# One hybrid encoder layer: 1/rms of the tokens spread over partitions by DMA through DRAM instead of TensorE, and four weight splits held until a late matmul

## The chip, the cores and the metric

The kernel runs on one core of a Trainium2 chip. The metric is the device time of one execution in microseconds. An execution is profiled as well; its trace gives every instruction of the five engines (PE is TensorE's matmul, PEld its weight load, DVE VectorE, ACT ScalarE, POOL GpSimd) and the DMA traffic. SP's queue only issues DMAs.

## The reference

One layer on 1,024 tokens of width 1,024, all in float32:

```
h = rms_norm(x, norm1_g)
u = h @ w_in                                  # conv (a, gate), q, k, v, g
a_out = conv_group(a * sigmoid(gate))         # causal depthwise conv(31), layer norm, silu
b_out = retention(rotary(q), rotary(k), v)    # chunked, 4 heads of 128, rms norm, * silu(g)
x = x + concat([a_out, b_out]) @ w_out
x = x + relu(rms_norm(x, norm2_g) @ w_ff1)**2 @ w_ff2
return rms_norm(x, final_g)
```

`rms_norm` multiplies each token by 1/sqrt(mean of its squares + eps). That one number per token is what the first part of the change moves about.

## The kernel before, in words

Each float32 matrix product is made of three products of rounded halves (`mm3`, L149 to L151): every operand is split into a high part `hi` (ACT copies it to the rounded type) and a low part `lo` (DVE subtracts). So each weight block needs one ACT and one DVE instruction before PE can use it. For w_in and w_out a block is loaded into `raw` (a pool of two buffers, L112), and split into `w` (L116 and L117, or L126 and L127 where a scale is multiplied in).

The tokens are not normalised before the first projection. x arrives transposed (`xcol`), is multiplied by norm1_g and split, and the factor 1/rms of a token, `r1`, is applied to the results. `stats` (L259 to L267) gets it: a block of 128 tokens `xt` is loaded with a token on each partition, ACT squares and sums it, POOL adds eps and takes the power -0.5. Where a result has tokens on partitions (q, k, v, g), `r1` is used as it is. The convolution's inputs (the gate tiles, `glu_proj` and `glu_gate`) have channels on partitions and tokens along the row, so there the factors have to stand as a row, the same on all 128 partitions: `r1_row`, one tile `row` of 128x512 for each half of the tokens. The kernel makes it with PE: POOL multiplies the identity by `r1` (`diag`, L351), PE multiplies by a matrix of ones (`pb`, L352), and ACT copies PSUM to `row` (L354). `pb` takes two buffers of the PSUM pool `pr` (four banks).

`glu_gate` does, for each half: `zg` (DVE, L294, accumulator times row), `sg` (ACT, sigmoid), `sr` (POOL, times row), `glu` (DVE, L299). It frees the PSUM banks of its gate tile. Four gate tiles j = 0 to 3 of 128 channels are made; j = 0 and 1 come first, then the projection of v (`wv`), then tiles 2 and 3, then k and q. The two half-tiles of j = 1 take banks of `pr`, those of j = 0 banks of `ps` (four banks), and the first group of v takes banks of `ps` that j = 0 held.

The convolution is 31 multiply-adds per channel tile on DVE (`y`, L395), spread over the whole first half of the kernel: each is put behind a matmul in the order of the program by a table (QUOTA). Such an entry, and `hold`, sets the order in which the scheduler places instructions; it adds no wait on the chip.

Retention handles the token blocks in pairs (`retention`, L438 to L480): PE transposes k and q (`pk`, `pq`), adds k times v to the running `pstate`, which ACT copies to `state` (L456) before the next block may add to it, makes the scores `psc` (L460), which DVE masks into `sT` (L462), and multiplies by v (`po`, L466 and L468). Between, PE works on the projection groups of q and of the gate g (`wg`, four groups of two blocks). The output projection starts with the retention half: `wo`, four row blocks of w_out multiplied by ret_norm_g (`load_wo(NC, True)`), then the convolution half `woa`.

The rest (feed-forward by a Strassen scheme) is not touched. Every engine carries out its instructions in order; an instruction that waits holds up what is queued behind it. `n2d` (L339) is a small DRAM tensor: SP's queue writes norm2_g to it, 1,024 separate numbers of 4 bytes, and `n2row` reads it back spread over the partitions.

Of the kernel before, what the change touches and what calls it, by code (L numbers as in the profile page):

```python
# [8 lines left out]
F32 = mybir.dt.float32  # L9
F32R = mybir.dt.float32r  # L10
BF16 = mybir.dt.bfloat16
AF = mybir.ActivationFunctionType
ALU = mybir.AluOpType
PSUM = bass.MemoryType.PSUM

P = 128
D = 1024
S = 1024
# [9 lines left out]
NC = CW // P  # L28
NF = FF // P
HALF = 512  # L30
# [11 lines left out]
def hybrid_layer_kernel(  # L42
# [14 lines left out]
    nc = tc.nc  # L57
# [6 lines left out]
    sp = pool("sp", 11)  # L64
    tiny = pool("tiny", 8)
    xd = pool("xd", 1, space=bass.MemoryType.DRAM)
# [3 lines left out]
    pr = pool("pr", 4, space=PSUM)  # L70
# [10 lines left out]
    ones = const.tile([P, P], F32, name="ones")  # L81
    nc.vector.memset(ones, 1.0)
    ident = const.tile([P, P], F32, name="ident")
# [12 lines left out]
    col = lambda nm, i: vec[:, cols[nm] + i : cols[nm] + i + 1]  # L96
# [9 lines left out]
    def load_raw(src, spare=False):  # L106

        if spare:
            raw = cp.tile(list(src.shape), F32, tag="c", name="raw")
        else:  # L110
            raw = rawp.tile(list(src.shape), F32, tag="raw", name="raw")
        nc.sync.dma_start(raw, src)  # L112
        return raw

    def split_row(raw, w, i):
        nc.scalar.activation(w[:, 0, i], raw[:, i], AF.Copy)  # L116
        nc.vector.tensor_tensor(w[:, 1, i], raw[:, i], w[:, 0, i].bitcast(F32), ALU.subtract)  # L117

    def split(raw, scales):

        w = wp.tile([P, 2] + list(raw.shape[1:]), F32R, tag="w", name="w")
        for i in range(raw.shape[1]) if scales else [slice(None)]:
            if scales is None:
                split_row(raw, w, i)
            else:
                nc.scalar.activation(w[:, 0, i], raw[:, i], AF.Copy, scale=scales[i])  # L126
                nc.vector.scalar_tensor_tensor(  # L127
                    w[:, 1, i], raw[:, i], scales[i], w[:, 0, i].bitcast(F32), ALU.mult, ALU.subtract
                )
        return w  # L130

    def load_split(src, scales):
        return split(load_raw(src), scales)

    pe_log, tap_log, act_log = [], [], []

    def hold(ins, until):

        name = lambda i: i.ins if hasattr(i, "ins") else i
        tc.add_manual_dep(  # L140
            name(ins),
            name(until).name,
            mybir.DependencyInfo(mybir.DependencyClass.NoSync, mybir.DependencyReason.DATA),
            reason="others first",
        )
# [15 lines left out]
    def mean_sq(src):  # L161

        tr = sp.tile([P, D], BF16, tag="s", name="trash")
        ss = tiny.tile([P, 1], F32, tag="ss1", name="ss")
        nc.scalar.activation(tr, src, AF.Square, scale=D**-0.5, accum_out=ss)
        return ss
# [43 lines left out]
    def chunk_w(c):  # L210
        return [load_split(w_in[c, i], None) for i in range(ND // 2)]
# [7 lines left out]
    def bank(i):  # L219

        if i % 2:
            return pr.tile([P, HALF], F32, tag="r", name="acc")
        return ps.tile([P, HALF], F32, tag="mm", name="acc")

    def proj_group(w, blocks, i=0):
        accs = [bank(i) for _ in blocks]
        for d in range(ND):
            for a, b in zip(accs, blocks):
                proj_tokens(w, b, a, d, d == 0, d == ND - 1)
        return accs  # L230

    r1, r1_pair = {}, None
# [22 lines left out]
    def stats(t):  # L255

        nonlocal r1_pair
        xt = cp.tile([P, D], F32, tag="c", name="xt")
        nc.sync.dma_start(xt, x[t * P : (t + 1) * P, :])  # L259
        if t % 2 == 0 or t >= 4:  # L260
            r1_pair = const.tile([P, 2], F32, name=f"r1_{t}")
            r1[t] = r1_pair[:, 0:1]
        else:
            r1[t] = r1_pair[:, 1:2]
        m = tiny.tile([P, 1], F32, tag="nmr", name="m1")
        nc.gpsimd.tensor_tensor(m, mean_sq(xt), eps1, ALU.add)
        nc.gpsimd.tensor_tensor(r1[t], m, mhalf[:, 0:1], ALU.pow)  # L267


    def glu_accs(j):  # L270
# [2 lines left out]
    def glu_proj(w, j, accs, d, h):  # L273

        for q in range(2):
            lo = (2 * j + q) * P
            mm3(
                accs[q][h],
                w[d // 2][:, 0, d % 2, lo : lo + P],
                w[d // 2][:, 1, d % 2, lo : lo + P],  # L280
                hT.half(d, 0, h),
                hT.half(d, 1, h),
                d == 0,
                d == ND - 1,
            )
# [31 lines left out]
    w = []  # L317
    accs = glu_accs(0)
    with tc.manual_schedule(engines=ordered):
# [6 lines left out]
        for i in range(ND // 2):  # L326
# [5 lines left out]
            for h in range(2):  # L332
                for d in (2 * i, 2 * i + 1):
                    glu_proj(w, 0, accs, d, h)
    nc.sync.dma_start(dec, decay)
    for t in range(NB):
        stats(t)
    n2d = xd.tile([D], F32, name="n2d")
# [2 lines left out]
    first, accs = accs, [[bank(1)], [bank(1)]]  # L341
# [3 lines left out]

    r1_row = []
    for h in range(2):
        pb = pr.tile([P, 4, P], F32, tag="r", name="pb")
        for i in range(4):
            diag = sp.tile([P, P], F32, tag="s", name="diag")  # L350
            nc.gpsimd.tensor_scalar(diag, ident, r1[4 * h + i], None, ALU.mult)  # L351
            nc.tensor.matmul(pb[:, i], lhsT=ones, rhs=diag, start=True, stop=True)  # L352
        row = sp.tile([P, HALF], F32, tag="s", name="row")
        nc.scalar.activation(row, pb.rearrange("p i t -> p (i t)"), AF.Copy)  # L354
        r1_row.append(row)
    nc.sync.dma_start(trg, trig)

# [16 lines left out]
    for g in range(NG):  # L374
        if g == NG - 1:
            w = chunk_w(2)
# [39 lines left out]
    w = wk  # L416
# [66 lines left out]
    def retain(waiting):  # L483
        runs = [retention(b, qr) for b, qr in waiting]
        for _ in range(3):
            for run in runs:
                next(run)
# [9 lines left out]

    marks.append(len(pe_log))

    def load_wo(first, scales):  # L500
        return [
            load_split(w_out[first + c].unsqueeze(1), [col("rg", c)] if scales else None) for c in range(NC)
        ]


# [20 lines left out]
    def ret_side(b):  # L526

        xr = [sp.tile([P, HALF], F32, tag="s", name="xr") for _ in range(2)]
        for n in range(2):
            nc.sync.dma_start(xr[n], x[b * P : (b + 1) * P, n * HALF : (n + 1) * HALF])  # L530
        pt = pr.tile([P, NC, P], F32, tag="r", name="pt")
        for c in range(NC):
            nc.tensor.transpose(out=pt[:, c], in_=blk[b][:, 0, c * P : (c + 1) * P], identity=ident)
        return split_tiles(pt), xr

    rsides = {}
    for g in range(NG):
        if g == NG - 1:
            wo = load_wo(NC, True)
        blocks = range(GB * g, GB * g + GB)  # L540
        accs = proj_group(wg, blocks)
        retain(waiting)
        waiting = []
        for b, acc in zip(blocks, accs):
            sg = sp.tile([P, CW], F32, tag="s", name="sg")
            nc.scalar.activation(sg, acc, AF.Silu, scale=r1[b])
            nc.vector.tensor_tensor(blk[b][:, 0], blk[b][:, 0], sg, ALU.mult)
            if b in (4, 5):
                rsides[b - 4] = ret_side(b - 4)
# [33 lines left out]
    for b in range(NB):  # L583
        if b + 2 < NB:
            rsides[b + 2] = ret_side(b + 2)
        if b == NB - 2:
            woa = load_wo(0, False)
        if b >= NB - 3:
            conv_norm(ORDER[b - (NB - 3)])
        if b >= NB - 2:  # L590
            conv_side(ORDER[b - (NB - 2)])
        (mh, ml), xr = rsides.pop(b)
        for n, acc in enumerate(out_proj(wo, mh, ml)):
            nc.vector.tensor_tensor(blk[b][:, n], acc, xr[n], ALU.add)
# [3 lines left out]
    i = 0  # L598
# [468 lines left out]
```

## Time and profile before

| what | value |
|---|---|
| median of 3 runs | 1042.36 us (1042.16 to 1043.71) |
| the profiled execution | 1042.16 us, of which 1040.2 us span from first to last instruction |
| PE busy | 1022.6 us, 98% |
| DVE busy | 800.8 us, 77% |
| ACT, POOL busy | 380.3 us, 139.5 us |
| PE's clock, granted | 0.999 of full speed |

The span is what the trace covers; some 2 us of the execution lie around it. Busy PE is an overlapped figure (a recorded matmul lasts 0.39 us but the next starts 0.23 us after it), so the table says only that PE hardly stands still. Where it does is read from the timeline: each row says in brackets how long the engine was idle before it, and what released it.

### The profile page before, as it was taken

Reading aid. Unit: us, or ns where it says so; the run is one execution under the profiler, and the core shown is the slowest. Engines: PE = TensorE matmul, PEld = TensorE weight load, DVE = VectorE, ACT = ScalarE, POOL = GpSimd, SP = SyncE. Lnnn points to the kernel's source line nnn. Section 1 sums busy time; section 2 is a strip of 40 time slices with the busy share of each in tenths; the row PEclk is TensorE's granted clock in tenths of the full one; section 3 lists DMA queues with packets and bytes.
Section 4 is the critical chain, followed back from the end, with each engine's and each line's share of the span. In section 5 each row is a group of like instructions: output and inputs, shape, how many; then the busy total and the mean of one; then the engine's idle time right before and its main releaser. Section 6 shows DMA issues by size and latency. Waiting matters only on the chain.

```text
span 1040.2 us, 12612 instructions
## 1 busy us (share of the span) xinstructions
PE 1022.6 (98%) x4726; PEld 849.0 (82%) x4726; DVE 800.8 (77%) x981; ACT 380.3 (37%) x596; POOL 139.5 (13%) x253
## 2 busy tenths in 40 slices
PE   9999999999999999999999999999999999999997
PEld 8788888898888877888888888887887888888885
DVE  6297777998797459997777767766998778778765
ACT  7511121034541366543233333333443333433442
POOL 0400110012100134112121211211100000000013
PEclk9999999999999999999999999999999999999999
DMA  9712021102042056565453443548565354255214
GB/s 359 161 62 81 4 78 42 41 21 82 4 148 91 21 198 219 204 224 186 143 193 142 158 166 122 176 169 299 178 207 195 102 182 164 99 186 178 89 54 162
DMA packets 52876, 145.38 MB, mean 140 GB/s; under 512 B 6864, under 2 KB 16208, under 8 KB 52816
## 3 DMA queue, kind: packets, MB, share of 16 engines
q1 hardware_dynamic: 38000, 107.35, 31.6%
q0 software_dynamic: 10592, 35.14, 8.6%
q10 hardware_dynamic: 4224, 2.10, 0.7%
q8 instruction: 37, 0.61, 0.2%
q14 instruction: 23, 0.19, 0.1%
HBM read 103.14 MB, written 41.42 MB: 139 GB/s over the span
## 4 chain that ended last, share of the span: by engine, by line
PE 84%; DVE 6%; DMA 4%; ACT 2%; issue 2%; SPq 1%; POOL 1%; ACTq 0%; POOLq 0%; DVEq 0%
PE acc L149 18%; PE acc L150 18%; PE acc L151 18%; PE pa L150 5%; PE pa L151 5%; PE pa L149 5%; PE pb L149 4%; PE pb L151 4%; PE pb L150 4%; DVE y L395 2%; DMA raw<-in_w_in_dram 2%; DMA w2raw<-in_w_dram 2%; DVE w L203 1%; DVE cols L253 1%; DVE w L117 1%
## 5 line engine op out<-in xcount | busy, mean ns | idle before, releaser
L149 PE MATMUL acc<-w 128*128 128x512 f32 x448 | 174.7, 390 | 1.8 <-DVE blk L939 1.0
L151 PE MATMUL acc<-w 128*128 128x512 f32 x448 | 174.3, 389 | 0.0
L150 PE MATMUL acc<-w 128*128 128x512 f32 x448 | 174.3, 389 | 0.0
L395 DVE SCALAR_TENSOR_TENSOR y<-glu,vec,y 128x1024 f32<-128x1024 f32 x120 | 153.7, 1289 | 2.0
L149 PEld LDWEIGHTS acc<-w 128*128 128x128 f32 x448 | 84.1, 188 | 20.7 <-issue 2.1
L149 PE MATMUL acc<-w,cols 128*128 128x512 f32 x256 | 100.1, 391 | 0.0
L150 PE MATMUL acc<-w,cols 128*128 128x512 f32 x256 | 99.8, 390 | 0.0
L151 PE MATMUL acc<-w,cols 128*128 128x512 f32 x256 | 99.7, 390 | 0.0
L151 PEld LDWEIGHTS acc<-w 128*128 128x128 f32 x448 | 84.1, 188 | 17.5
L150 PEld LDWEIGHTS acc<-w 128*128 128x128 f32 x448 | 84.1, 188 | 17.2
L200 ACT ACTIVATE w<-xr 128x1024 fp32r<-128x1024 f32 x56 | 59.3, 1058 | 97.9 <-PE acc L151 42.9
L203 DVE TENSOR_TENSOR w<-xr,w 128x1024 fp32r<-128x1024 f32 x56 | 68.3, 1220 | 28.3 <-ACT w L200 27.8
L939 DVE TENSOR_TENSOR blk<-acc,blk 128x512 f32<-128x512 f32 (+1 forms) x113 | 72.8, 680 | 17.0 <-PE acc L151 17.0
L149 PE MATMUL pb<-h,w1h 128*128 128x512 f32 x192 | 74.9, 390 | 0.4 <-DVE h L203 0.4
L151 PE MATMUL pa<-h,w1l 128*128 128x512 f32 x192 | 74.9, 391 | 0.0
L149 PE MATMUL pa<-h,w1h 128*128 128x512 f32 x192 | 74.7, 392 | 0.0
L150 PE MATMUL pb<-h,w1h 128*128 128x512 f32 x192 | 74.7, 389 | 0.0
L151 PE MATMUL pb<-h,w1l 128*128 128x512 f32 x192 | 74.7, 389 | 0.0
L203 DVE TENSOR_TENSOR w1l<-t,w1h 128x1024 fp32r<-128x1024 f32 x32 | 39.2, 1224 | 43.4 <-PE pb L150 40.1
L116 ACT ACTIVATE w<-raw 128x1024 fp32r<-128x1024 f32 (+1 forms) x32 | 30.5, 955 | 85.9 <-PE acc L151 70.2
L151 PEld LDWEIGHTS acc<-w,cols 128*128 128x128 f32 x256 | 48.1, 188 | 10.0
L149 PEld LDWEIGHTS acc<-w,cols 128*128 128x128 f32 x256 | 48.1, 188 | 9.8
(186 smaller groups left out, 2008.7 us busy)
## 6 DMA issues: line engine op xcount, KB each, us to landing
w1raw<-in_w_dram SPq DMA_DIRECT2D x32, 512.0 KB, 4.6
w2raw<-in_w_dram SPq DMA_DIRECT2D x32, 512.0 KB, 4.6
raw<-in_w_in_dram SPq DMA_DIRECT2D x23, 512.0 KB, 3.3
xt<-in_x_dram SPq DMA_DIRECT2D x8, 512.0 KB, 7.5
raw<-in_w_out_dram SPq DMA_DIRECT2D x8, 512.0 KB, 3.3
xr<-in_x_dram SPq DMA_DIRECT2D x16, 256.0 KB, 2.9
kept<-blk POOLq DMA_DIRECT2D x8, 512.0 KB, 3.7
blk<-kept SPq DMA_DIRECT2D x8, 512.0 KB, 4.7
```

The costliest lines, as they stand in the source:

```text
L116: nc.scalar.activation(w[:, 0, i], raw[:, i], AF.Copy)
L117: nc.vector.tensor_tensor(w[:, 1, i], raw[:, i], w[:, 0, i].bitcast(F32), ALU.subtract)
L149: nc.tensor.matmul(acc, lhsT=lh, rhs=rh, start=first, stop=False, **kw)
L150: nc.tensor.matmul(acc, lhsT=lh, rhs=rl, start=False, stop=False, **kw)
L151: pe_log.append(nc.tensor.matmul(acc, lhsT=ll, rhs=rh, start=False, stop=last, **kw))
L200: act = nc.scalar.activation(hi, src, AF.Copy)
L203: nc.vector.tensor_tensor(lo, src, hi.bitcast(F32), ALU.subtract)
L253: nc.vector.scalar_tensor_tensor(lo, raw[:, i], col("n1", d), hi.bitcast(F32), ALU.mult, ALU.subtract)
L395: nc.vector.scalar_tensor_tensor(y, glu[c][:, k : k + S], tap(k), y, ALU.mult, ALU.add)
L939: return nc.vector.tensor_tensor(t, acc[lane][r][:, lo:hi], t, ALU.add)
```

## The change

First, the 1/rms rows. `stats` now ends with a DMA from POOL's queue that writes the 128 factors to a DRAM tensor `r1d`, one number of 4 bytes from each partition. Each `row` is filled by another DMA from POOL's queue, which reads 512 factors and gives them to all 128 partitions. `diag`, `pb` and the copies from PSUM are gone, and with them the two banks of `pr`.

Second, `load_wo` for the retention half gets the last matmul logged so far, that of the third gate group, as `until`: ACT's half of each of the four splits is placed after it in the order.

```diff
-    def split(raw, scales):
+    def split(raw, scales, until=None):
...
-                nc.scalar.activation(w[:, 0, i], raw[:, i], AF.Copy, scale=scales[i])
+                n = nc.scalar.activation(w[:, 0, i], raw[:, i], AF.Copy, scale=scales[i])
+                if until is not None:
+                    hold(n, until)
...
         nc.gpsimd.tensor_tensor(r1[t], m, mhalf[:, 0:1], ALU.pow)
+        nc.gpsimd.dma_start(r1d[t * P : (t + 1) * P].unsqueeze(1), r1[t])
...
+    r1d = xd.tile([S], F32, name="r1d")
     for t in range(NB):
         stats(t)
...
     for h in range(2):
-        pb = pr.tile([P, 4, P], F32, tag="r", name="pb")
-        for i in range(4):
-            diag = sp.tile([P, P], F32, tag="s", name="diag")
-            nc.gpsimd.tensor_scalar(diag, ident, r1[4 * h + i], None, ALU.mult)
-            nc.tensor.matmul(pb[:, i], lhsT=ones, rhs=diag, start=True, stop=True)
         row = sp.tile([P, HALF], F32, tag="s", name="row")
-        nc.scalar.activation(row, pb.rearrange("p i t -> p (i t)"), AF.Copy)
+        nc.gpsimd.dma_start(row, r1d[h * HALF : (h + 1) * HALF].partition_broadcast(P))
         r1_row.append(row)
...
-            wo = load_wo(NC, True)
+            wo = load_wo(NC, True, pe_log[-1])
```

The scheduler orders the engines anew. Three places matter. POOL at the end of the statistics, before (line numbers of the kernel before) and now (lines have moved by two or three):

```order
L266 TENSOR_TENSOR m_369<-ss,eps_96 128x1
L267 TENSOR_TENSOR r_6_368<-m_369,mhalf 128x1
L351 TENSOR_SCALAR diag<-ident,r_0_316 128x128 x2
L351 TENSOR_SCALAR diag<-ident,r_2_333 128x128 x2
L266 TENSOR_TENSOR m_378<-ss,eps_96 128x1
L267 TENSOR_TENSOR r_7_377<-m_378,mhalf 128x1
L351 TENSOR_SCALAR diag<-ident,r_4_350 128x128
```

```order
L268 TENSOR_TENSOR m_376<-ss,eps_96 128x1
L269 TENSOR_TENSOR r_6_375<-m_376,mhalf 128x1
L270 DMA r1d<-r_6_375 128x1
L353 DMA row<-r1d 128x512
L268 TENSOR_TENSOR m_386<-ss,eps_96 128x1
L269 TENSOR_TENSOR r_7_385<-m_386,mhalf 128x1
L270 DMA r1d<-r_7_385 128x1
L353 DMA row<-r1d 128x512
L301 TENSOR_TENSOR sr<-sg,row 128x512 x8
```

The load of the first row stands ahead of the last block's factor; POOL waits there until the writes that it reads have landed, and again at the second. `sr` comes behind both.

DVE at the first gate tile, before and now (the names after the arrow are what is read):

```order
L294 TENSOR_TENSOR zg<-acc,row 128x512
L117 TENSOR_TENSOR w<-raw,w 128x1024
L294 TENSOR_TENSOR zg<-acc,row 128x512
L299 TENSOR_TENSOR glu<-acc,sr 128x512
L117 TENSOR_TENSOR w<-raw,w 128x1024
L299 TENSOR_TENSOR glu<-acc,sr 128x512
```

```order
L297 TENSOR_TENSOR zg<-acc,row 128x512
L117 TENSOR_TENSOR w<-raw,w 128x1024
L302 TENSOR_TENSOR glu<-acc,sr 128x512
L297 TENSOR_TENSOR zg<-acc,row 128x512
L117 TENSOR_TENSOR w<-raw,w 128x1024
L297 TENSOR_TENSOR zg<-acc,row 128x512
L302 TENSOR_TENSOR glu<-acc,sr 128x512 x2
```

The second half's `zg` has moved behind the first half's `glu`.

DVE at the retention of the third pair, where the first split of `wo` stood (L127), before and now:

```order
L117 TENSOR_TENSOR w<-raw,w 128x1024
L395 SCALAR_TENSOR_TENSOR y<-glu,vec,y 128x1024
L127 SCALAR_TENSOR_TENSOR w<-raw,vec,w 128x1024
L462 TENSOR_TENSOR sT<-psc,dec 128x512
L395 SCALAR_TENSOR_TENSOR y<-glu,vec,y 128x1024
L462 TENSOR_TENSOR sT<-psc,dec 128x512
```

```order
L117 TENSOR_TENSOR w<-raw,w 128x1024
L394 SCALAR_TENSOR_TENSOR y<-glu,vec,y 128x1024 x2
L461 TENSOR_TENSOR sT<-psc,dec 128x512
L394 SCALAR_TENSOR_TENSOR y<-glu,vec,y 128x1024
L461 TENSOR_TENSOR sT<-psc,dec 128x512
```

In the split's place stands one more multiply-add of the convolution. On ACT the split's other half (L126) is gone from ahead of the copy of `pstate`.

## Rows read from the trace of the kernel before

**Rows 1.** The page: busy us, share of the span and instructions of each engine.

```profile
PE 1022.6 (98%) x4726; PEld 849.0 (82%) x4726; DVE 800.8 (77%) x981; ACT 380.3 (37%) x596; POOL 139.5 (13%) x253
```

**Rows 2.** Timeline of PE, 39 to 54 us: start, duration, instruction, [idle before <-releaser].

```profile
39.38 1.95 PE L352 MATMUL pb<-diag,ones 128*128 128x128 f32 x16
...
41.18 0.50 PE L149 MATMUL acc<-cols,w 128*128 128x512 f32 x1
...
42.20 0.39 PE L150 MATMUL acc<-cols,w 128*128 128x512 f32 x1
...
43.45 0.50 PE L149 MATMUL acc<-cols,w 128*128 128x512 f32 x1 [0.86 <-ACT row L354]
...
53.35 0.39 PE L149 MATMUL acc<-w,cols 128*128 128x512 f32 x1
```

**Rows 3.** Timeline of PE, 247 to 253 us.

```profile
247.43 0.83 PE L460 MATMUL psc<-qT,kT 128*128 128x128 f32 x6
...
250.07 1.16 PE L451 MATMUL pstate<-blk 128*128 128x128 f32 x8 [1.80 <-ACT state L456]
...
251.06 1.28 PE L460 MATMUL psc<-qT,kT 128*128 128x128 f32 x10
...
252.90 0.49 PE L466 MATMUL po<-blk,sT 128*128 128x128 f32 x2 [0.33 <-DVE sT L462]
```

**Rows 4.** Timelines of ACT and DVE, 248 to 253 us.

```profile
248.38 1.15 ACT L126 ACTIVATE w<-raw,vec 128x1024 fp32r<-128x1024 f32 x1 [1.85 <-DMA raw<-in_w_out_dram]
...
249.78 1.28 DVE L395 SCALAR_TENSOR_TENSOR y<-glu,vec,y 128x1024 f32<-128x1024 f32 x1
...
250.97 1.28 DVE L127 SCALAR_TENSOR_TENSOR w<-raw,vec,w 128x1024 fp32r<-128x1024 f32 x1
...
252.17 0.68 DVE L462 TENSOR_TENSOR sT<-psc,dec 128x512 f32<-128x512 f32 x1
```

**Rows 5.** Timeline of ACT, 41 to 46 us.

```profile
41.85 1.06 ACT L116 ACTIVATE w<-raw 128x1024 fp32r<-128x1024 f32 x1 [0.72 <-DMA raw<-in_w_in_dram]
...
44.71 0.63 ACT L296 ACTIVATE sg<-zg 128x512 f32<-128x512 f32 x1
```

**Rows 6.** Timeline of DVE, 49 us.

```profile
49.33 0.68 DVE L299 TENSOR_TENSOR glu<-acc,sr 128x512 f32<-128x512 f32 x1
```

**Rows 7.** Timeline of POOL, 23 to 47 us.

```profile
23.66 0.19 POOL L266 TENSOR_TENSOR m<-ss,eps 128x1 f32<-128x1 f32 x1 [22.29 <-ACT trash L165]
...
23.93 0.55 POOL L267 TENSOR_TENSOR r<-m,mhalf 128x1 f32<-128x1 f32 x1
...
45.42 1.30 POOL L298 TENSOR_TENSOR sr<-sg,row 128x512 f32<-128x512 f32 x1 [7.90 <-PE acc L151]
```

**Rows 8.** Line 741, DMAs that POOL issues: ns min/median/max of one; landing.

```profile
L741 POOL DMA_DIRECT2D x1M<-hid x6: 539/542/542, 438.7 to 502.7; - x6
...
DMA to landing us min/median/max: 2.2/2.7/8.0
```

**Rows 9.** Lines 339 (n2d), 620 (n2row), 964 (fg): landing of their DMAs.

```profile
DMA to landing us min/median/max: 16.0/16.0/16.0
...
DMA to landing us min/median/max: 3.5/3.5/3.5
...
DMA to landing us min/median/max: 5.6/5.7/5.8
```

**Rows 10.** Stretches: us, engines' busy time, clock, DMA share, GB/s.

```profile
24.00:31.00 7.00, 7.00 (x33) 5.79 (x32) 0.00 (x0) 6.37 (x12) 4.44 (x15) 1.00 1.15 387
31.00:40.00 9.00, 9.00 (x44) 7.56 (x43) 0.00 (x0) 1.26 (x4) 6.18 (x12) 1.00 0.94 78
```

**Rows 11.** Timeline of PE, 297 to 310 us.

```profile
297.04 0.39 PE L151 MATMUL acc<-w,cols 128*128 128x512 f32 x1
...
309.40 0.48 PE L149 MATMUL acc<-w,mh 128*128 128x512 f32 x1
```

**Rows 12.** The page: DMA issues, KB each, median us to landing.

```profile
raw<-in_w_out_dram SPq DMA_DIRECT2D x8, 512.0 KB, 3.3
```

More of the change, by code (lines that the diff above doesn't have):

```diff
@@ L130, in split, with load_split @@
         return w
-    def load_split(src, scales):
-        return split(load_raw(src), scales)
+    def load_split(src, scales, until=None):
+        return split(load_raw(src), scales, until)
     pe_log, tap_log, act_log = [], [], []
@@ L498, in hybrid_layer_kernel, with load_wo @@
     marks.append(len(pe_log))
-    def load_wo(first, scales):
+    def load_wo(first, scales, until=None):
         return [
-            load_split(w_out[first + c].unsqueeze(1), [col("rg", c)] if scales else None) for c in range(NC)
+            load_split(w_out[first + c].unsqueeze(1), [col("rg", c)] if scales else None, until) for c in range(NC)
         ]
```

## The prediction, written before the changed kernel ran

> **What bounds the kernel now.** I read the page's busy shares first, then the waits of PE, then the stretches around the two places that the change touches. PE is busy for 1022.6 of 1040.2 us of span [rows 1], so only time in which PE works on something that can go, or stands still, can be won. The profiled execution took 1042.16 us with 1.96 us around its span; the median of the three runs, 1042.36, is 0.2 above it, so a saving read from this trace is taken off 1042.4.
>
> First place, 39 to 53 us [rows 2]: the second gate tile (j = 1) has finished its half h = 0. PE then makes `pb` (16 recorded 128x128 matmuls), begins five matmuls of half h = 1, and stops for 0.86 us until ACT's second `row` copy (L354) has freed a PSUM bank. Behind that half stands the projection of v, from 53.35. Second place, 247 to 253 us [rows 3, 4]: ACT is in order, and its split of the first `w_out` row block (L126) waited 1.85 us for a DMA. The copy of `pstate` stands behind it, and PE loses 1.80 us, then 0.33 at `po`, which needs DVE's `sT`.
>
> **Part A, what goes.** From the start of `pb` to the first matmul of h = 1: 41.18 - 39.38 = 1.80 us. From 42.20 to 43.45 there are 1.25 us where one matmul step is due; the 43 matmuls from 43.45 to 53.35 take 0.23 each, so 1.02 is lost. Sum 2.8 us [rows 2]; ACT's two row copies and POOL's eight `diag` go as well, off the path. In the changed order h = 1 waits for nothing but PE. PE would be at the v projection at 39.4 + 48 x 0.23 = 50.45 in place of 53.35, so 2.9 us with the ragged restart.
>
> **What takes its place.** The v projection starts when three things are there: the first v weights split, and two PSUM banks that `glu_gate(first)` frees, the second of them by `glu` of h = 1 (PE's fourth matmul, so 50.45 + 3 x 0.23 = 51.1). That gate needs both rows, which now come by DMA. Two clocks run toward 51.1.
>
> Clock 1, the weights. ACT's first v split ran at 41.85, when its load landed, then the row copy and the sigmoid table, then `sg` at 44.71, and DVE's second `glu` began 49.33 and ended 50.0 [rows 5, 6]. The changed order takes the 0.6 us row copy out from between, so `sg` can start about 44.2; but it puts the second `zg` behind the first `glu`. From there: sg 0.63, sr 1.30, glu 0.68, zg (two operands of the same shape) 0.68, sg 0.63, sr 1.30, glu 0.68 = 5.9 and some 0.6 of hand-overs [rows 5 to 7]: 50.7. That is 0.4 before 51.1, so **no wait, if the load lands when it did**.
>
> Clock 2, the rows. POOL per block of 128 tokens: m 0.19, pow 0.55, issue of the new write 0.54 (as an issue on its queue costs elsewhere), gaps of 0.1 each, and one more while ACT's result is taken up: 1.65 us [rows 7, 8]. From 23.66 seven blocks and the four memsets (0.4) end at 35.6. The first row's load stands there in line, waits for writes 0 to 3 (issued by 30), and is out at 36.2; block 7's write is out at 37.8. Landing of a 128 x 4 byte write to DRAM: no such row. POOL's quickest DRAM writes land in 2.2 us; the nearest in kind is `n2d`, 1,024 writes of 4 bytes, 16.0 us [rows 8, 9], of which about 7 are the queue behind the `xt` loads (still 387 GB/s until 31 us) and 9 its own: between 31 and 40 us the engines moved 78 GB/s [rows 10] with more loads waiting. An eighth of 9 is 1.1, so I take 2.2 + 1.1 = 3.3 (bounds 2.2 and 16). Block 7 is in DRAM at 41.1; POOL waited for that, issues the second row by 41.7, and a 128-partition broadcast lands in 3.5 us as `n2row` did [rows 9]: **45.2**. From it zg, sg, sr, glu are 3.3 + 0.3, so anything up to 47.5 costs nothing. The first row lands about 39.7; it has to be there by 42.6, or the table load and `sg` slip. Queued behind the waiting POOL is only `sr`, due at 44.8; behind DVE's waiting `zg` the v split's second half.
>
> By the `n2d` row alone the write would land 16 us after its issue, the second row at 58 and the sum would be 10 us slower. Against that speaks the queue: `n2d` stood behind `xt` on SP's queue, the new writes are on POOL's. The Trainium skill, page "DMA: Bandwidth & Descriptors", section "Queues, rings and completion order", says that each DMA engine takes turns between the queues that have work, packet by packet; by that the 7 us do not apply and the sum is the one above. No run here shows it yet for small writes.
>
> Does the new traffic hold up clock 1? The eight writes are together as many 4-byte packets as `n2d`. Bounds: 0 us, if bursts of 128 are swallowed, and 9 us, if each holds the engines for its share of `n2d`'s 9. I take 0.2 beyond the 0.4 of slack: while the `xt` loads ran at 387 GB/s to 31 us the first of `n2d`'s packets were already in that stretch, and a burst is an eighth of it. This is the softest number here.
>
> **Part B, the held splits.** The four splits of `wo` move from before (one in the retention at 248 us, three later) to after PE's 297.04, the last matmul of the third gate group [rows 11]. On ACT nothing then stands before the state copy, and PE's 1.80 goes. But `po` needs `sT` from DVE, which runs in one unbroken row there: y at 249.78, the split's low half at 250.97, sT at 252.17, po at 252.90 [rows 3, 4]. In the changed order a second `y` stands where the low half stood; a y that reads the one before it starts after that one's whole 1.28, not after 1.19. So `sT` comes at about 252.3 and PE, which could be there at 250.35 (247.43, 24 steps of 128 columns at 0.11, one matmul of 0.23), waits at `po` instead: **0 won, 0.1 lost**. Bounds: 2.6 won (252.90 - 250.35) if DVE got there early; a loss if the late splits reach the output projection late. That: high half of split 0 done 298.5, low half 299.8, the third block's load issued then, landed in 3.3 us [rows 12], high half 304.4, low half 306.6; the fourth by 309.1. Its matmul is 9 after 309.40, so 311.5 [rows 11]: 2.4 us of cover, made of the last gate group's 48 matmuls. Without it PE would wait for the rest. The `y` taps that move ahead fill time in which DVE waited, and the loads of the other half of `w_out` go late by some 10 us, needed only about 345.
>
> **Sum.** -2.9 + 0.2 + 0.1 = -2.6: **1039.8 us**.
>
> **Rivals.**
> 1. The rows come late, and the time is unchanged. Write 3 goes out at 30, when `n2d`'s writes have filled the way; if it lands only at 40 when they are through, the first row's load is issued then, block 7 behind it on POOL is out at 42.1, lands 45.4, the second row lands 49.5 to 51.7 (3.5 us as `n2row`, or 5.7 as `fg`, a broadcast on a busier way [rows 9]). PE waits for 49.5 + 3.6 - 51.1 = 2.0 to 4.2: 1041.6 to 1043.8. For it: 78 GB/s from 31 to 40 [rows 10]. Against: only 8 small writes per engine have to get through.
> 2. Slower: the small writes hold the DMA engines as `n2d` did, and the first v weights come late. In full, 9 us: ACT's split at 50.9 instead of 41.85, the second `glu` at 59.7, PE waits 8.6: 1042.4 - 2.9 + 8.6 = 1048.1. It decides from 3.3 us of delay on, that is from a landing after 45.2. For it: 4 KB of `n2d` cost the queue 9 us. The Trainium skill, same page, section "Specifications", says that below 512 B an engine reads, modifies and writes; by that each new write costs its engine what one of `n2d`'s cost, which is this case. The trace agrees as far as `n2d` goes; it shows no burst of 128.
> 3. Part B does what its name says, DVE reaching `sT` early: 2.5 better, 1037.3. Against it stands DVE's unbroken row.
>
> **How the numbers follow.** A measurement here can tell about 0.2%, 2.1 us, from no change. Forecast 0.38 (1039.3 to 1040.3), rival 3 0.05, together faster 0.43; rival 1 and the mild end of rival 2 0.31, same; rival 2 from 3.3 + 2 us of delay on, 0.26, slower. The range leaves out rival 3 and the worst of rival 2: 1039.0 to 1047.0.
>
> **What would show it.** Part A right: no idle of PE at 42 and at most half a us ahead of the first v matmul, which stands near 50.5; landing of `row` before 47.5. Rival 1: DVE's `zg` or POOL's row load waits for DMA, PE waits for `glu`. Rival 2: the first v split on ACT waits for its load beyond 43. Part B: the wait of `pstate` gone and one of some 2.5 us at `po` in its place; no wait in the output projection from 309 on. I am wrong if PE reaches the v projection late by more than 1 us, or if DVE's row before `sT` is shorter than before.

## The result, and the profile after

The changed kernel is slower by 1%: 1052.83 us (median of four runs, 1050.29 to 1054.93) against 1042.53 (1042.16 to 1043.71) for the kernel before, a ratio of 1.0104 with a 95% interval of 1.0088 to 1.0120. The forecast was 1039.8, and the range ended at 1047.0. The profiled execution took 1051.20 us with a span of 1048.9 (before: 1042.16 and 1040.2); the lines below are from it. Line numbers from 120 on lie some 2 to 4 away from those before.

The page's first row still says that PE is the bound; it answers to [rows 1], and such a share hides 9 us that stand in one place:

```profile
PE 1023.3 (98%) x4710; PEld 847.9 (81%) x4710; DVE 798.5 (76%) x981; ACT 378.8 (36%) x594; POOL 139.7 (13%) x255
```

PE's timeline around the v projection (start, duration, instruction, idle before it and what ended that), where [rows 2] stood:

```profile
50.08 0.39 PE L151 MATMUL acc<-w,cols 128*128 128x512 f32 x1
50.48 0.50 PE L152 MATMUL acc<-w,cols 128*128 128x512 f32 x1
50.82 0.40 PE L153 MATMUL acc<-w,cols 128*128 128x512 f32 x1
58.10 0.80 PE L151 MATMUL acc<-w,cols 128*128 128x512 f32 x1 [6.88 <-DVE glu L302]
58.69 0.63 PE L152 MATMUL acc<-w,cols 128*128 128x512 f32 x1
...
66.55 0.50 PE L152 MATMUL acc<-w,cols 128*128 128x512 f32 x1 [1.56 <-DVE w L117]
```

PE arrives at 50.08, not at 53.35: 3.3 us won. After three matmuls it stands until 58.10, for the bank that `glu` of the first half frees; from 64.59 to 66.55 it stands once more, 1.95 us from one start to the next, for DVE's half of a weight split, which is queued on DVE behind the second half's `zg` and `glu`. The stretches behind the stand (third number from the end: PE's granted clock):

```profile
54.00:56.00 2.00, 0.00 (x0) 0.00 (x0) 0.00 (x0) 0.00 (x0) 0.52 (x1) 0.66 0.33 23
56.00:58.00 2.00, 0.00 (x0) 0.00 (x0) 0.65 (x1) 0.00 (x0) 1.30 (x2) 0.50 0.52 162
58.00:60.00 2.00, 1.90 (x5) 1.53 (x6) 0.05 (x1) 0.00 (x0) 0.00 (x0) 0.50 0.59 168
60.00:62.00 2.00, 2.00 (x7) 1.48 (x6) 1.90 (x3) 0.63 (x1) 0.40 (x1) 0.64 0.00 0
```

The clock fell to 0.50, the lower of its two levels (1.2 of 2.4 GHz), while PE stood, and came back at about 61.4: the eight steps from 58.10 to 61.59 take 3.49 us where 1.81 are due. So the projection of v lost 7.05 (first stand) + 1.7 (clock) + 1.7 (second stand) + 0.3 (ragged start) = 10.7 of the 10.9 by which it fell back, from 3.3 early to 7.7 late.

Who was late is read from POOL's timeline, which answers to [rows 7]:

```profile
29.62 0.58 POOL L270 DMA_DIRECT2D r1d<-r  x1 [0.29 <-POOL r L269]
...
36.29 0.58 POOL L270 DMA_DIRECT2D r1d<-r  x1 [0.29 <-POOL r L269]
45.09 0.55 POOL L353 DMA_DIRECT2D row<-r1d  x1 [8.22 <-DMA r1d<-r]
45.66 0.20 POOL L268 TENSOR_TENSOR m<-ss,eps 128x1 f32<-128x1 f32 x1
45.94 0.56 POOL L269 TENSOR_TENSOR r<-m,mhalf 128x1 f32<-128x1 f32 x1
46.79 0.58 POOL L270 DMA_DIRECT2D r1d<-r  x1 [0.29 <-POOL r L269]
55.48 0.55 POOL L353 DMA_DIRECT2D row<-r1d  x1 [8.11 <-DMA r1d<-r]
56.05 1.27 POOL L301 TENSOR_TENSOR sr<-sg,row 128x512 f32<-128x512 f32 x1
```

Block 3's write left at 29.62 and held the first row's load until 45.09. Behind that load, on the same engine, stood block 7's factor and its write; that write left at 46.79 and held the second row's load until 55.48; and behind that load stood `sr`, ready to go since about 51.3, which PE was waiting for through `glu`. The landings of the writes (line 270) and of the row loads (line 353):

```profile
DMA to landing us min/median/max: 8.4/12.3/15.2
...
DMA to landing us min/median/max: 3.4/4.0/4.5
```

ACT's timeline (it answers to [rows 5]) shows the first v split, 2.8 us later than before. DVE's shows its waits for the rows and for POOL:

```profile
44.66 1.06 ACT L116 ACTIVATE w<-raw 128x1024 fp32r<-128x1024 f32 x1 [6.85 <-DMA raw<-in_w_in_dram]
```

```profile
48.60 0.69 DVE L297 TENSOR_TENSOR zg<-acc,row 128x512 f32<-128x512 f32 x1 [25.99 <-DMA row<-r1d]
...
57.35 0.69 DVE L302 TENSOR_TENSOR glu<-acc,sr 128x512 f32<-128x512 f32 x1 [6.93 <-POOL sr L301]
60.10 0.69 DVE L297 TENSOR_TENSOR zg<-acc,row 128x512 f32<-128x512 f32 x1 [2.06 <-DMA row<-r1d]
```

At the second place PE's timeline, where [rows 3] stood, reads

```profile
257.76 0.48 PE L151 MATMUL acc<-w,cols 128*128 128x512 f32 x1
260.67 0.49 PE L465 MATMUL po<-blk,sT 128*128 128x128 f32 x2 [2.44 <-DVE sT L461]
```

The wait of `pstate` is gone, and `po` waits 2.44 us for `sT`: PE, 7.67 us late before this place, is 7.77 late behind it. Nothing waits in the output projection (7.76 at the end of the last gate group). From 394 to 455 us, in the first feed-forward stage, another 2 us go, and some 1.2 come back later; more of that below.

### The profile page after: what moved, and what is told of

Same layout as the page of the kernel before. It is cut to its first block, busy times and chain, and to the rows that moved or that the text cites. A ratio compares the mean times of both kernels' runs of the same rounds, so it can differ in the third digit from the quotient of the medians.

```text
span 1048.9 us, 12576 instructions
## 1 busy us (share of the span) xinstructions
PE 1023.3 (98%) x4710; PEld 847.9 (81%) x4710; DVE 798.5 (76%) x981; ACT 378.8 (36%) x594; POOL 139.7 (13%) x255
## 4 chain that ended last, share of the span: by engine, by line
PE 83%; DMA 5%; DVE 5%; ACT 2%; issue 2%; POOL 1%; SPq 0%; POOLq 0%; ACTq 0%; DVEq 0%
PE acc L151 18%; PE acc L152 18%; PE acc L153 18%; PE pa L153 5%; PE pa L151 5%; PE pa L152 5%; PE pb L151 4%; PE pb L153 4%; PE pb L152 4%; DVE y L394 2%; DMA r1d<-r 1%; DMA raw<-in_w_in_dram 1%; DMA w2raw<-in_w_dram 1%; DMA h<-colsT 1%; DMA xt<-in_x_dram 1%
## 5 line engine op out<-in xcount | busy, mean ns | idle before, releaser
L205 DVE TENSOR_TENSOR w1l<-t,w1h 128x1024 fp32r<-128x1024 f32 x32 | 39.1, 1223 | 43.4 <-PE pb L152 40.1
```

What stands on the lines that cost most here:

```text
L205: nc.vector.tensor_tensor(lo, src, hi.bitcast(F32), ALU.subtract)
```

## The experiments

**My theory after the result.** The whole loss is part A's; its cause is the landing of a 128 x 4 byte write, waited for twice in series. Rival: part B has a share. For the writes there are three rivals more: `n2d`'s traffic, POOL's queue, and the sharing of DRAM lines. On the chips of these runs the kernel before took 1039.9 to 1040.7 (medians), and each ratio is to the runs of before on the same chip.

**e1, part B alone; e2, part A alone.** e1 is the kernel before with `until` in `split`, `load_split` and `load_wo`; e2 is the changed kernel with

```
-            wo = load_wo(NC, True, pe_log[-1])
+            wo = load_wo(NC, True)
```

> Part B alone: the four splits held to the gate, with the factors still spread by TensorE. Theory (the trace of after: the wait of pstate for ACT is gone, po waits 2.4 us for DVE's sT in its place): the kernel before plus 0.1 us, 1042.5, a ratio within 0.999 to 1.001; PE waits for sT, none at pstate. Rival (rival 3 of the prediction, hidden in the changed kernel by the loss at the v projection): 2.5 us faster, 1040. Second rival (the loss of 10 us has a share here, late splits at the output projection): slower by over 1 us.

> Part A alone: the rows spread by DMA, the splits of w_out where they were before. Theory (the whole loss is from part A): the time of the changed kernel, 1050 to 1055, with PE standing some 7 us before the v projection and its granted clock near 0.5 behind that. Rival: part B has a share of the loss and this kernel is 1 us or more quicker than the changed one on the same chip, fast runs against fast runs.

e1: 1040.71 us, ratio 1.0002 (0.9993 to 1.0011). e2: 1051.04, ratio 1.0091 (1.0071 to 1.0112); in its trace PE stands 7.0 us at the same place, with the clock at 0.50 behind that. So part A has the loss and part B is worth nothing, by the measure of its runs. e1's trace shows one thing that I had not expected, in the stretches behind the wait at `po`:

```profile
250.00:254.00 4.00, 1.61 (x13) 1.30 (x12) 3.96 (x5) 0.00 (x0) 0.00 (x0) 0.99 0.39 131
254.00:256.00 2.00, 2.00 (x11) 2.00 (x11) 2.00 (x3) 0.00 (x0) 0.00 (x0) 0.50 0.00 0
256.00:258.00 2.00, 2.00 (x14) 2.00 (x13) 1.97 (x3) 0.88 (x7) 0.00 (x0) 0.66 0.00 0
```

Part B makes one stand of 2.9 us (from start to start) out of two, of 2.1 and 0.8. Behind it the clock fell to 0.50 here, and PE lost 1.6 us more. Of the other eight traces with part B and its stand of 2.9 us, those of e3, e4 and e5 show the same, and those of the changed kernel, e6, e8, e14 and e15 show 1.00 throughout. So it comes in some executions only.

**e3, one landing in place of two.** Both row loads go behind block 7's write (`writes` lists the eight writes):

```
-        nc.gpsimd.dma_start(row, r1d[...].partition_broadcast(P))
+        hold(nc.gpsimd.dma_start(row, r1d[...].partition_broadcast(P)), writes[-1])
```

> The changed kernel with one thing moved: POOL issues both row loads behind the write of block 7, so that the landing of a write is waited for once and not twice in a row. Theory (two landings of 8 us in series on POOL, the first holding block 7's factor, its write and sr): block 7's write goes out at 38, lands 46.5 to 48, the rows 3.5 to 4.5 later at 50.5 to 52.5, zg, table load, sg, sr and glu after that end at 55.5 to 57.5; PE waits 4.5 to 6.5 us in place of 7.3, and the second wait of 1.95 us is gone: 1 to 4 us quicker than the changed kernel, still slower than before by 5 to 9. Rival (the single landing decides, whoever waits in line): no difference to the changed kernel. Rival (the writes need a rate, not a latency: 1,024 of them at some 12 ns or more each): block 7's write lands still later than 48 as it then stands behind the other seven.

1046.99 us, ratio 1.0059 (1.0044 to 1.0074). POOL's timeline:

```profile
39.78 0.58 POOL L270 DMA_DIRECT2D r1d<-r  x1 [0.29 <-POOL r L269]
46.62 0.55 POOL L354 DMA_DIRECT2D row<-r1d  x1 [6.26 <-DMA r1d<-r]
47.52 0.54 POOL L354 DMA_DIRECT2D row<-r1d  x1 [0.35 <-issue]
```

Block 7's write lands 7.2 us after its issue here, at 47.0; block 3's, issued at 30.04, lands 16.0 us after its own, at 46.0, and that is what the first row's load waited for. So both loads leave within 0.9 us of each other, and the rest of the stand is the price of that one landing; the stands of PE at v shrink to 1.2, 1.0 and 2.65 us from start to start, with the clock at half behind them too. Against e2, which stands for the changed kernel on this chip, the series of two waits was 3.2 points in a thousand of the ratio, about a third of the loss; the two intervals are wide (1.0071 to 1.0112, 1.0044 to 1.0074), so the share is rough.

**What makes the landing long: e5, e6, e8, e14, e15.** Each is the changed kernel with the form of the write, its queue or its neighbour changed.

```
changed: dma_start(r1d[t * P : (t + 1) * P].unsqueeze(1), r1[t])         r1d [S]
e5       dma_start(r1d[t * P : (t + 1) * P, 0:1], r1[t])                 r1d [S, P]
e14      dma_start(r1d[t * P : (t + 1) * P], wide)                       r1d [S, P], wide = ones * r1[t], 128x128
e15      dma_start(r1d[t * P : t * P + 16].unsqueeze(1), r1[t][0:16])    r1d [S]
e8       (nc.sync if t == NB - 1 else nc.gpsimd).dma_start(...)          the rest as changed
e6       the line of n2d's DMA moved down to n2row                       the rest as changed
```

In e5 and e15 one more DMA at the start fills with ones what the row loads read, and in e5 and e14 a row load reads four lines of 512 bytes.

> The changed kernel, with each factor written to the start of a 512-byte line of its own in DRAM; the row loads read lines that are filled with ones at the start (but for each block's first factor), so the factors along the rows are not the true ones. Everything else, counts and sizes of writes and loads too, is as in the changed kernel. Theory (a write of 128 x 4 bytes lands late because its 128 small writes go to the same few lines one behind another): block 7's write, alone on quiet DMA engines, lands 2 to 4 us after its issue in place of 8.4, the row loads wait less, PE's stand at the v projection falls below 3 us. Rival (small size by itself, wherever it goes): landing 7 to 10 us and PE's stand of 7 us as in the changed kernel.

> The changed kernel, with the transfer n2d (1,024 writes of 4 bytes) issued only just before its reader, hundreds of us later. Theory (each of the small writes is slow by itself; n2d adds traffic among the first seven of them alone): the writes of blocks 0 to 3 land some us earlier, the first row load goes out 3 to 6 us earlier than at 45.1, block 7's write and the second row as much earlier; block 7's write still takes 7 to 9 us; PE's stand falls from 7.3 us to 1 to 5 us, and the time lies 2 to 7 us under the changed kernel, still above before. Rival 1 of the prediction (n2d's writes fill the way, without them a landing takes 2 to 3 us): rows by 46, no stand, 1039 to 1041. Other rival (n2d plays no part): 1050 to 1053 as the changed kernel.

> The changed kernel, with the write of block 7 alone issued by SyncE in place of GpSimd. Theory (the landing time belongs to the form of the write and not to the queue of GpSimd): it lands 7 to 10 us after its issue, as the 8.4 us from GpSimd; SyncE stands until block 7's factor is there, so loads behind it (the weights) go later; PE stands 5 to 9 us at the v projection. Rival (it is GpSimd's queue, with descriptors made by software, that is slow): it lands in 2 to 3 us, and the second row comes some 5 us earlier than in the changed kernel.

> The changed kernel, with each factor written 128 times side by side, so that a write is 128 whole lines of 512 bytes, 64 KB in place of 512 bytes; POOL makes the 128 x 128 tile first, 0.4 us; the row loads read one line of each block, so the factors along the rows are not the true ones. Theory (the size of 4 bytes makes the landing slow, in the same line or not): the last write, alone, lands 2 to 3.5 us after its issue in place of 8.4, and PE's stand at the v projection is under 2 us. Rival (a write from 128 partitions to DRAM lands late at any size): 4.5 us or more.

> The changed kernel, with 16 of each block's 128 factors written (16 writes of 4 bytes in one 64-byte stretch), the rest of the row's scratch filled with ones at the start, so the factors along the rows are not the true ones. Theory (the landing grows with the number of small writes that go to neighbouring places, some 40 to 50 ns each): the last write lands 2 to 3.5 us after its issue in place of 8.4. Rival (a small write has its 7 us whatever their number): 6 us or more.

The last write, block 7's, is the cleanest of the eight: the loads of `xt` and `n2d` are through, and the first row's load is issued just ahead of it. The DMA issues between 44 and 56 us (out<-in, queue, KB, median us to landing) of the changed kernel, e15, e5, e8 and e14:

```profile
r1d<-r POOLq DMA_DIRECT2D x1, 0.5 KB, 8.4
```

```profile
r1d<-r POOLq DMA_DIRECT2D x1, 0.1 KB, 1.8
```

```profile
r1d<-r POOLq DMA_DIRECT2D x1, 0.5 KB, 4.6
```

```profile
r1d<-r SPq DMA_DIRECT2D x1, 0.5 KB, 7.2
```

```profile
r1d<-wide POOLq DMA_DIRECT2D x1, 64.0 KB, 5.8
```

Sixteen writes of 4 bytes to one stretch of 64 bytes land in 1.8 us, 128 to one stretch of 512 bytes in 8.4. From SyncE the 128 land in 7.2, so it is not POOL's queue. In lines of their own they land in 4.6, whole lines of 512 bytes in 5.8; my expectations of 2 to 4 and 2 to 3.5 fell. What is left in those two is the first row's load. It goes in pieces of 512 bytes there and itself takes 6.4 us to land, and the write's packets come behind its own. The DMA packets of the changed kernel from 46.8 to 48.4 and from 48.4 to 55.2 us (block 7's write left at 46.79 and landed at 55.2):

```profile
DMA packets 89, 0.17 MB, mean 105 GB/s; under 512 B 48, under 2 KB 48, under 8 KB 89
```

```profile
DMA packets 28, 0.13 MB, mean 19 GB/s; under 512 B 0, under 2 KB 0, under 8 KB 27
```

and those of e5 from 45 to 47.5 and from 47.5 to 49.3 us (its write left at 45.05 and landed at 49.7):

```profile
DMA packets 39, 0.16 MB, mean 64 GB/s; under 512 B 0, under 2 KB 0, under 8 KB 39
```

```profile
DMA packets 64, 0.07 MB, mean 37 GB/s; under 512 B 48, under 2 KB 48, under 8 KB 64
```

The 48 small packets are 32 of the write and 16 that close the row's load. In the changed kernel they are all over 1.6 us after the write's issue, and the landing comes 6.8 us behind them; in e8 it comes 5.5 us behind (48.6 and 54.1). In e5 the packets go late, but the landing is there 0.4 us after 49.3; in e14 and e15 it is there within 0.5 us too (49.5 and 49.9, 45.0 and 45.5). So by these traces neither the size of 4 bytes nor the number of 128 makes the last write land late: it is 128 small writes into one stretch of 512 bytes. Whether the number of writes in the stretch or its length counts, these runs do not separate, and e5, e8, e14 and e15 are one run each.

The first wait has another part. With 16 factors a write, block 3's write in e15 still landed 11.4 us after its issue, against 14.9 in the changed kernel, and the first row's load left at 41.93, against 45.09. The packets of SP's queue (q1) and POOL's (q0) in the changed kernel from 24 to 36 us, and of POOL's from 36 to 45:

```profile
q1 hardware_dynamic: 1767, 2.65, 117.6%
q0 software_dynamic: 66, 0.00, 0.5%
```

```profile
q0 software_dynamic: 158, 0.00, 2.2%
```

POOL's are the first seven writes, 32 packets each. Six of them were issued by 34 us, yet only 66 of the 224 packets had gone by 36; on SP's queue `n2d` and the loads of `xt`, `trg` and the weights were under way. How much of this is `n2d` no run shows, since none takes it away from there.

e15 took 1041.98 us, 1.5 more than the kernel before on its chip. PE waited 1.2 us at v, for a split of weights, in place of 6.9 and 1.6, and was 2.2 us ahead behind it: with the last landing short and the first row's load 3 us earlier, the loss at v is gone. The others took 1051.67 (e5), 1048.17 (e8) and 1046.74 us (e14). e5 lost 3.1 us less than the changed kernel at v, but its clock fell to 0.50 behind `po` and again at 404 us.

For `n2d`, e6: 1048.89 us, ratio 1.0088 (1.0073 to 1.0103). The move put `n2d` only 3 us later (issued at 26.2, landed 18.7 later, at 44.9), so it doesn't take it away from the first seven writes. But the last one left behind it:

```profile
46.32 0.58 POOL L270 DMA_DIRECT2D r1d<-r  x1 [0.29 <-POOL r L269]
54.38 0.55 POOL L352 DMA_DIRECT2D row<-r1d  x1 [7.48 <-DMA r1d<-r]
```

and its load waited nearly as long. Rival 1 of the prediction had the rows late at the right place. Its reason, `n2d` in the way, is not the last write's; for the first wait it is neither shown nor refuted.

**e4 and e9, a better form.** The factors of a half's four blocks stand in four columns of one tile, DVE turns squares of 32 x 32, and one write for each half carries rows of 128 bytes:

```
...
         row = sp.tile([P, HALF], F32, tag="s", name="row")
-        nc.gpsimd.dma_start(row, r1d[h * HALF : (h + 1) * HALF].partition_broadcast(P))
+        nc.vector.transpose(row[:, 0:32], r1_cols[h])
+        nc.gpsimd.dma_start(r1d[h].rearrange("(c g j) -> g c j", g=4, j=32), row[:, 0:32])
+        nc.gpsimd.dma_start(row, r1d[h][0:HALF].partition_broadcast(P))
...
```

e9 is e4 without part B.

> The changed kernel, with the form of the writes changed: the eight factors of a half stand side by side in one tile, DVE turns it in squares of 32 by 32, and one write for each half of 128 partitions with 128 bytes each (its used part 16 rows of 128 bytes) takes the place of four writes of 128 x 4 bytes; the row loads are as they were. Theory (it is writes of 4 bytes that land late): the two writes land within 2 to 4 us of their issue near 37 to 38, the rows by 42 to 46, PE doesn't wait at the v projection, no fall of the clock, and the time is that of the forecast, 1039 to 1040.5, faster than before. Rival (any small write to DRAM from this queue lands 8 us or more after its issue at this place, or n2d's writes hold it up): rows at 48 to 52, PE waits 2 to 6 us, 1042 to 1049.

> The kernel with turned factors (two writes of 128 x 128 bytes), without the held splits. Theory (the held splits make one stand of 2.9 us at the po of the first gate group out of two of 2.1 and 0.8, and behind the longer stand the granted clock falls, 1.7 us; without them it doesn't): the 3.3 us won at the v projection stay, no clock under 1.00 at 240 to 260 us, and the time is 2 to 3.5 us under before, ratio 0.9965 to 0.998. Rival (the gain is given back by a later stage whatever stands in between, as at 446 us, where the kernel with both parts waited 1.6 us for the load of h): ratio 0.999 to 1.001, with PE's lead of 3.3 us lost again by 460 us.

e4: 1042.21 us, ratio 1.0015 (1.0006 to 1.0024). e9: 1040.73, ratio 1.0007 (0.9996 to 1.0017). I had expected both to be faster than before; neither is. The two writes take 7.4 to 9.3 us in e4, with `n2d` under way, so my term for them was too small again. But they leave at 32.6 and 34.9 and are waited for together. In e9 the second `zg` runs at 47.71 with a wait of 0.19, and PE goes through the v projection without a stand, 3.2 us ahead. Its profiled execution was the quickest of twelve, 1037.51, 2.4 us under the median of before on its chip, near the gain that was forecast for the change; the median shows nothing of it. Hence four more runs.

**e10, e11, e12, e13: where the lead goes.** e11 is the kernel before, and e12 e9, both unchanged; e10 is e9 with `n2d`'s line moved as in e6; e13 is e9 with the other scratch tiles in DRAM allocated ahead of `r1d`.

> The turned factors without the held splits, and n2d's 1,024 small writes moved to just before their reader. Theory (the kernel with turned factors alone has almost no slack at the v projection: its second glu ended near 50.8 where 51 is needed, so executions in which the rows land a little later stand there, and its median shows little of the 3.3 us that its profiled execution won; without n2d ahead of them the two writes land 2 to 5 us earlier): rows by 43, ACT's table load and sg then wait for the weights and no more for the rows, and the median is 2.5 to 3.5 us under before, 0.9965 to 0.9976. Rival (what is given back is lost later, in the stages from 300 us on, and not at the rows): ratio 0.999 to 1.001 again though the rows come earlier.

> The kernel before, unchanged, for a second trace of it beside those of this chip: it shows what differs from execution to execution with nothing changed. If the stages from 300 us on differ by 1 to 2 us between its two traces, such differences of the other traces there are no effect of an edit.

> The turned factors without the held splits once more, for a second trace (the first was of the quickest of its executions, 1037.5, where the median was 1040.7). Theory (no slack at the rows): where this execution takes 1040 or more, PE stands 1 to 3 us at the v projection, and its granted clock is under 1.00 there. Rival: PE leads by 3.3 us behind the v projection and loses it at 390 to 460 us, where a load of the first feed-forward stage lands late.

> The turned factors without the held splits, and nothing else changed but the place of their scratch in DRAM: the other scratch tiles are allocated first, so that they lie where they lay in the kernel before. Theory (the shifted places of the scratch tiles make the loads at 383 to 450 us collide more often): the weight load at 383 us lands within 4 us, no loss at 394 and 446, and the median is 2 to 3.5 us under before, ratio 0.9966 to 0.998. Rival (the loads there land late or not for another reason, such as the moment at which PE and the queues arrive): ratio 0.9995 to 1.0015, as for the same kernel with the scratch in front.

e10: 1041.21 us, ratio 1.0011 (1.0002 to 1.0020). e13: 1040.03, ratio 0.9997 (0.9988 to 1.0005). One run each: e11 1039.72, e12 1041.75. In e10 `n2d` left only 2 us later than in e9, the two writes landed 10.8 and 8.7 us after their issue, and the rows came no earlier (the first `zg` at 47.43, in e9 at 45.70). PE's place against e11, from the traces (minus is ahead), and how long after its issue at about 382 to 385 us DVE had a weight load of the feed-forward stage (`w1raw`):

| trace | start of v | at 390 us | that load, us | behind 455 us |
|---|---|---|---|---|
| before, first trace | -0.2 | -0.2 | 5.0 | +1.1 |
| e9 | -3.2 | -3.1 | 3.8 | -3.1 |
| e12 | -3.5 | -2.4 | 5.3 | +1.4 |
| e10 | -3.7 | -2.9 | 5.5 | -0.3 |
| e13 | -3.1 | -2.7 | 6.2 | +1.7 |
| e4 | -3.5 | -1.8 | 5.2 | +1.7 |

In e11 itself the load took 3.4 us. DVE's row for it in e9 and in e12:

```profile
385.85 0.69 DVE L699 TENSOR_TENSOR t<-w1raw 128x512 f32<-128x512 f32 x1 [1.68 <-DMA w1raw<-in_w_dram]
```

```profile
388.11 0.70 DVE L699 TENSOR_TENSOR t<-w1raw 128x512 f32<-128x512 f32 x1 [3.24 <-DMA w1raw<-in_w_dram]
```

and PE in e12, sixty us on, where the load of `h` is late as well:

```profile
445.71 0.44 PE L153 MATMUL pa<-h,w1l 128*128 128x512 f32 x1
447.64 0.73 PE L151 MATMUL pa<-h,w1h 128*128 128x512 f32 x2 [1.49 <-ACT h L202]
```

(On the way to 390 us, e12 and e10 lost 1.1 and 0.8 us within the v projection, where a half of a weight split came late, and e4 lost 1.6 by the clock behind `po`.) So the lead is real and is lost some 340 us later, where the load lands 5.2 to 6.2 us after its issue in four of these five traces; the kernel before had the first of these losses in one of its two traces. "No slack at the rows" does not explain it: what e10 and e12 lost at v is under a third of the lead. The place of the scratch in DRAM is refuted by e13. An early PE is not what it takes: the load of this place took 4.7 to 6.0 us also in the changed kernel, e3, e5, e6, e8 and e14, where PE was late, and 4.0 in e1 and e2. Why it lands late in so many traces stays open; none of the versions beats the kernel before.

## Why the prediction was wrong

- **PE's arrival at v: right.** 50.45 was said, 50.08 came; 2.9 us were said to be won, 3.3 were.
- **POOL's share for a block: nearly right.** 1.65 us were taken, 1.73 measured (26.15, 27.89, 29.62, 31.35): between the factor and the issue of its write lies 0.3 where I took 0.1.
- **Landing of the write: the step that failed.** I took 3.3 us between bounds of 2.2 and 16, since an eighth of `n2d`'s own 9 us came to 1.1. It was 8.4 to 15.2, and 8.4 for the last, with nothing of `n2d` left. The 9 us do not shrink with the number of writes alone. In the trace of the kernel before, `n2d` lands at 40.1; the packets from 28 to 33 and from 33 to 40.2 us are

```profile
DMA packets 1355, 1.15 MB, mean 230 GB/s; under 512 B 1075, under 2 KB 1075, under 8 KB 1355
```

```profile
DMA packets 181, 0.64 MB, mean 89 GB/s; under 512 B 24, under 2 KB 24, under 8 KB 181
```

so nearly all its 1,024 small packets are over by 33, and 7 us pass behind them, as 6.8 pass behind the 128 writes of block 7. `n2d` puts 128 writes into each of eight stretches of 512 bytes, a factor write puts 128 into one; 16 in 64 bytes took 1.8 us in all. As an estimate, 6.8 us for 128 is 53 ns a write, and 7 us for the 128 of each of `n2d`'s stretches is 55: that would fit writes into one stretch which land one behind another, and stretches side by side. No run tests it. The range of the landing held what came; my choice of value did not, and I had not carried the upper bound of 16 into the range of the time.

- **The price by the `n2d` row, set aside: nearest.** By that row alone the prediction had the second row at 58 and a sum 10 us slower than 1039.8; the row came at 60.0, and the time was 1052.83. I set it aside because the new writes stand on a queue of their own. That did not spare them: of the first seven writes' packets only 66 of 224 had gone by 36 us.
- **What that price does: twice, not once.** "Block 7's write is out at 37.8" rested on the first row's load going out at 36.2. It went at 45.09, and block 7's factor, its write and `sr` stood behind it on POOL. I had named `sr` as queued there, and that block 7 is behind the first row's load, but priced one late landing. With e3's order the series is gone and the ratio falls from 1.0104 (1.0091 in e2) to 1.0059.
- **Which `glu` PE needs: wrong, without weight in the sum.** PE's fourth matmul of v was to need the second half's `glu`. It began at 58.10, behind the first half's `glu` (57.35); the second half's comes only at 63.12.
- **The clock: not foreseen.** 1.7 us of the loss at v.
- **Weights for v (rival 2): half right.** The first split came 2.8 us late, at 44.66, against 0.2 taken. It goes with the form of the writes: the split came at 44.9 to 46.3 in e2, e3 and e8, which have the same writes, and at 41.6 to 42.0 in e5, e14 and e15 (in e6, with `n2d` behind that load, at 42.19). The delay is one that rival 2 had named; it is under the 3.3 from which it would have decided, and the rows were later still.
- **Part B: right.** 0.1 lost was said, 0.1 measured, with the wait of 2.5 us at `po` in place of `pstate`'s; that the clock can fall behind it, 1.6 us, was not said.
- **The rivals.** The way was rival 1's (rows late, POOL's load waiting), with a size that rival 1 didn't have: the second row came near 60 us, not at 49.5 to 51.7. The chance for slower stood on rival 2 alone.

The Trainium skill, page "DMA: Bandwidth & Descriptors", section "Anatomy of one DMA — SWDGE (gpsimd) path", puts a fixed cost of about 2.0 us on a transfer, most of it the receipt of the write. e15's 1.8 us agrees; the 8.4 us for 128 writes of 4 bytes into one stretch doesn't, and there the measurement decides. The same page's section "Issuing engines are not separate DMA queues" says that another issuing engine saves only issuing time; e8's 7.2 us from SyncE agrees.

## What to carry to other kernels

A transfer to DRAM of one small element from each of 128 partitions is to be priced by a row of its own kind and not by its bytes: here 512 bytes in one stretch took longer to land (8.4 us) than a 256 KB broadcast (3.4 to 4.5), and in lines of their own the same writes landed 0.4 us behind their packets. Where a queue's next instruction waits for a landing, write out everything behind it on that engine and price the landing once for each wait in the chain; putting the waiting loads behind all the writes won about a third of the loss. And a few us won at one place show in the median only if the stages behind it keep them: look at a second trace before believing the first.

## What the runs showed of the hardware that was not expected

- 16 writes of 4 bytes to one 64-byte stretch of DRAM landed in 1.8 us, 128 to one stretch of 512 bytes in 7.2 to 8.4 (block 7's in the changed kernel, e2, e3, e6 and e8), 128 to lines of their own in 4.6 behind a load. Between the last small packet and the landing lay 6.8 us in the changed kernel and 5.5 in e8, but 0.4 to 0.5 in e5 and e15.
- Behind stands of PE of 7.3 us (the changed kernel) and 2.9 us (e1, e3, e4, e5) the granted clock was 0.50 until 3.4 to 4.3 us after work began again; behind the same stand of 2.9 us it stayed 1.00 in five other traces, the changed kernel's among them. This cost 1.6 to 1.7 us each time.
- A load of 512 KB in the first feed-forward stage took 3.4 or 5.0 us in two executions of the same kernel, and PE lost 1.3 us by it.
